# A GLA tile's output: turned by VectorE and stored by four transfers in place of TensorE, and the first out products in blocks of three

## The chip, the core and the metric

The kernel runs on one core of a Trainium2 chip. A core has five engines that run their own instruction queues beside each other: TensorE (PE in the profile, with its weight loads as PEld), VectorE (DVE), ScalarE (ACT), GpSimd (POOL) and SyncE (SP), which here issues nearly all DMA transfers. The metric is the device time of one execution in microseconds; a kernel's time is the median of its runs.

## The reference

One layer of a hybrid decoder, for a prompt of 2048 positions and 8 x 8 sampled positions, in float32. What bears on the change:

```
h    = RMSNorm(x);  proj = h @ w_in          # split into attention and GLA columns
attn = sliding-window attention with sinks    # 512 columns
# gated linear attention (GLA): 4 heads, dk 64, dv 128, log decays log_a per position and key
o    = causal GLA output, S = state carried from position to position
o    = rms_norm(o, g_gla) * silu(gr)          # per head of 128 columns
mix  = concat([attn, o]) @ w_out              # 1024 x 1024
x    = x + rms_norm(mix, g_mix_post)
x    = x + rms_norm((relu(RMSNorm(x) @ w_up))^2 @ w_down, g_ffn_post)
```

## The kernel before

The prompt is cut into tiles of 128 positions, 0 to 15; tile 16 (`NB`) holds the 64 sampled positions. Every float32 product is made of three products of float32r parts (high x high, high x low, low x high), so an operand is split before it is used: ACT copies the high part, DVE subtracts it for the low part.

The stages follow each other on TensorE: attention tiles (to about 310 us), GLA tiles (to about 670), output projection of the remaining tiles (to about 830), then the two MLP halves. The change is in the GLA stage and at its border to the output projection.

**A GLA tile.** `gla(i, gp, og)` is a generator. It computes decays with ACT and DVE (`level_sums`), weights keys and queries by them (`weighted_keys`, `weighted_queries`), has PE multiply them level by level into `gl` and `gh`, has DVE place those into a matrix AH under masks (`put_level`), copies that into AT, and has PE form the output from AT and the values and from the old state S (`o<-gp,AT`, `o<-S,qd`, and the same into the bank `ds`). The keys weighted to the tile's end (`kdT`) are turned by DVE in blocks of 32 x 32 and by way of memory: `keys_turn` transposes the blocks into `blocks`, stores four parts to `kd_d` and loads `kd` back. The next tile's queries and keys are turned in the same manner (`turn`).

**What runs between.** Each `yield n, free` of `gla` lets PE run n matmuls out of a long generator `fill`: the input projections of later tiles (`gproj`, by `products`), and at its end the first products of the output projection (`out`). The list `G_FILL` says how many stand at each place. `te`, `ac`, `dv` and `sq` wrap an engine so that its instructions stay in the order in which the program issues them; `sq` is SP's queue.

**The tile's output.** `finish_out(i, ...)` runs inside the next tile, `gla(i + 1)`, which steps it by `next(og)` and empties it by `deque(og, 0)`: squares on ACT, the inverse root on POOL, four DVE instructions into `og` (positions x columns). The output projection needs columns on partitions, so `og` is transposed: four PE transposes into a PSUM bank of kind "e" (`ogT`), an ACT copy to `mo`, one store to `mix_d[i][:, 4:8]`. The bank of kind "e" is also the one that the next tile's `o` takes. Tiles 15 and 16 do it in a branch of their own.

**The border to the output projection.** `products` ends with tile 15's projection, chunk by chunk. When a chunk of w_in has been used for the last time, its place takes parts of w_out: `load_wo` issues the loads of `wo` for columns 0 to 511, and after the last chunk `load_wo_half` those for columns 512 to 1023, two gains and `mt_raw`, the mix tile of tile 1. The parts of w_out were split and stored to `wo_d` in earlier tiles, one of eight per tile (`split_wo`, instructions `wop<-wor`). Mix tiles 0 and 4 (`B_ORDER[:2]`) are placed at the first chunk, and `split_mix(..., True)` puts their high parts into the list `highs` and their low parts, in halves, into `lows`; `gla` takes from these lists at fixed places with `take`. Then `out_projecting` for the two tiles runs in turns of two products:

```python
order[: 3 * KT] = [
    (0, k, u) for s in range(KT + 4) for k, u in ((s, 0), (s, 1), (s - 4, 2)) if 0 <= k < KT
]
```

so the products that need the low part of a mix tile (u = 2) come four k behind the others. The other mix tiles are loaded by `load_mix` and split by one ACT and one DVE instruction.

Of the kernel before, what the change touches and what calls it, by code (L numbers as in the profile page):

```python
# [12 lines left out]
F32 = mybir.dt.float32  # L13
F32R = mybir.dt.float32r
U8 = mybir.dt.uint8
AF = mybir.ActivationFunctionType
ALU = mybir.AluOpType
# [4 lines left out]
P = 128  # L22
D = 1024
KT = D // P
T = 2048
NB = T // P
# [54 lines left out]
B_ORDER = (*(j + b for j in range(4) for b in (0, 4)), NB, *(j + b for j in range(4) for b in (8, 12)))  # L81
# [47 lines left out]
def f32(ap):  # L129
    return ap.bitcast(F32)  # L130
# [23 lines left out]
def hybrid_step_kernel(ctx: ExitStack, tc: tile.TileContext, I, O):  # L154
# [10 lines left out]
    def rows(i):  # L165
        return min(P, NTOK - i * P)
# [7 lines left out]
    te, ac, dv, sq = (InOrder(tc, engine) for engine in (nc.tensor, nc.scalar, nc.vector, nc.sync))  # L174
# [17 lines left out]
    mix_d = [dpool.tile([P, KT, rows(i)], F32, name=f"mix_d{i}") for i in range(NTILE)]  # L192
# [36 lines left out]
    def split_copy(hi, lo, src, vector=nc.vector):  # L229

        nc.scalar.activation(hi, src, AF.Copy)
        return vector.tensor_tensor(lo, src, f32(hi), op=ALU.subtract)  # L232
# [52 lines left out]
    sp = open_pool("a_s")  # L285
# [583 lines left out]
    early, late = (deque((c, k) for c in cs for k in range(KT)) for cs in (G_EARLY, G_LATE))  # L869
# [21 lines left out]
    for i in range(NB):  # L891
# [21 lines left out]
        if i >= NB - 2:  # L913
            t = i - NB + 2
# [121 lines left out]
    sp = open_pool("g_s")  # L1036

    def places(name, shape, n=1, kind=F32):
        return cycle([sp.tile(shape, kind, name=f"{name}{u}") for u in range(n)])
# [3 lines left out]
    AT = sp.tile([P, 4, P], F32, name="AT")  # L1043
    AH = sp.tile([P, 4, HD], F32, name="AH")
    kds = places("kd", [P, 256], 2)
    ogs, mos = places("og", [P, 4, P]), places("mo", [P, 4, P])
    XK = sp.tile([P, NL, 2, P], F32, name="XK")
    XQ = sp.tile([P, NL, 2, 2, P // 2], F32, name="XQ")
    sgs = places("sg", [P, 512])
# [116 lines left out]
    def weighted_keys(xk, dec, kt, l, b, vector):  # L1166

        if l:
            vector.tensor_tensor(pairs(xk[:, l], b, 0), pairs(dec[:, l], b, 0), pairs(kt, b, 0), op=ALU.mult)
# [51 lines left out]
    def put_diagonal(i, at, gp, n, vector=dv):  # L1221
# [7 lines left out]
        shape = [n, 4, HD]  # L1229
        vector.copy_predicated(at, dmsk[:n].unsqueeze(1).to_broadcast(shape), dg[:n].unsqueeze(2).to_broadcast(shape))  # L1230

    def finish_out(i, og_src, sg, n, kind):

        ssq = sp.tile([P, 4], F32, tag="ossq", name=f"ossq_{i}", bufs=2)
        junk = sp.tile([P, P], mybir.dt.bfloat16, tag="ojunk", name=f"ojunk_{i}", bufs=1)
        scalar, vector = (ac, dv) if i < NB else (nc.scalar, nc.vector)
        for h in range(4):
            scalar.activation(junk[:n], og_src(h), AF.Square, accum_out=ssq[:n, h : h + 1])
            if i < NB - 1 and h in (0, 1, 3):
                yield  # L1240
        rs = sp.tile([P, 4], F32, tag="ors", name=f"ors_{i}", bufs=2)
        rsqrt_mean(sp, rs[:n], ssq[:n], n, P, 4, vector)
        if i < NB - 1:
            yield
        if i == NB:
            yield 44, True
            yield 44, True
        og = next(ogs) if i < NB else gp_s[:, :512].rearrange("p (h d) -> p h d", h=4)
        for h in range(4):
            with tc.issue_after(put[0].ins) if i == NB else nullcontext():  # L1250
                vector.scalar_tensor_tensor(
                    og[:n, h, :], og_src(h), rs[:n, h : h + 1], sg[:n, h * P : (h + 1) * P],
                    op0=ALU.mult, op1=ALU.mult,
                )
        for _ in range(S_WAIT[0] if i == NB else 1):
            yield 34, True
        pt = bank([P, 4, P], kind, f"ogT_{i}")
        for h in range(4):
            te.transpose(pt[:, h, :n], og[:n, h, :], ident[:n, :n])
        if i == NB - 1:  # L1260
            hi, lo = late_mix
            dv.tensor_copy(hi, pt)
            dv.tensor_tensor(lo, pt, f32(hi), op=ALU.subtract)
        elif i < NB - 1:
            mo = next(mos)
            ac.activation(mo, pt, AF.Copy)
            sq.dma_start(mix_d[i][:, 4:8, :], mo)
        else:
            nc.scalar.activation(gp_s[:, :256].rearrange("p (h t) -> p h t", h=4), pt[:, :, :n], AF.Copy)
            sq.dma_start(mix_d[i][:, 4:8, :], gp_s[:, :256].rearrange("p (h t) -> p h t", h=4))  # L1270
# [15 lines left out]
    def gla(i, gp, og=iter(())):  # L1286
# [20 lines left out]
        for l, b in enumerate(LEVELS[3:6], 3):  # L1307
            level_sums(before, after, dec, l, b)
            next(diagonal, None)
            take(lows, l % 2)  # L1310
            if l > 3:
                next(og, None)
            yield next(fills), False
        for l in (1, 2, 3):
            weighted_keys(XK, dec, kt, l, LEVELS[l], dv)
        ac.activation(edge, before[:, :, HD - 1 :: HD], AF.Copy, scale=1.0 / 16)
        whole(kdT, after, 0)
        dv.tensor_tensor(kdT, kdT, kt, op=ALU.mult)
        take(lows, 1)
        take(x_loads)  # L1320
        if i < NB - 1:
            keys_turn(i, kdT, kd)
# [8 lines left out]
        for l in (0, 1):  # L1331
            weighted_queries(XQ, dec, qz, l, LEVELS[l], dv)
        next(og, None)
        take(lows)
        yield next(fills), False
        level_sums(before, after, dec, NL - 1, LEVELS[-1])
        whole(dec[:, NL], before, 1)
# [28 lines left out]
        take(put_off)  # L1366
        yield next(fills), False
        deque(og, 0)
        yield next(fills), True
        yield next(fills), True  # L1370
        low = bank([P, 4, 4, P // 4], "c", f"gl_{i}")
# [38 lines left out]
        for g in range(2):  # L1410
            dv.scalar_tensor_tensor(
                Sn[:, g], So[:, g], dec[:, NL, g, P - 1 : P], ds[:, g], op0=ALU.mult, op1=ALU.add
            )
        yield next(fills), True
        for h in range(4):
            te.matmul(
# [99 lines left out]

    def split_mix(i, m, ks, raw, apart=False):
        n = rows(i)
        if apart:
            hi, lo = m[:, 1], m[:, 2]  # L1520
            highs.append(lambda: ac.activation(hi, raw, AF.Copy))
            for k in range(0, KT, 4):
                kk = slice(k, k + 4)
                lows.insert(
                    len(lows) if k else len(lows) // 2,
                    lambda kk=kk: dv.tensor_tensor(lo[:, kk], raw[:, kk], f32(hi[:, kk]), op=ALU.subtract),
                )
            return [[m[:, u, k, :n] for k in range(ks)] for u in (1, 2)]
        if i == NB:
            split_copy(m[:, 1, :, :NS], m[:, 1, :, NS:], raw[:, :, :NS])  # L1530
            return m[:, 1], None
        split_copy(m[:, 1, :ks, :n], m[:, 2, :ks, :n], raw[:, :ks, :n])
        parts = [[m[:, u, k, :n] for k in range(ks)] for u in (1, 2)]
        if i == NB - 1:
            for t, late in zip(parts, late_mix):
                t.extend(late[:, h, :] for h in range(4))
        return parts

    def load_mix(i):
        return split_mix(*place_mix(i))  # L1540

    def out_projecting(te, i, banks):

        mh, ml = mixes.pop(i, None) or load_mix(i)
        n, ends = 2 if i == NB else 3, range(2)
        order = [(c, k, u) for c in ends for k in range(KT) for u in range(n)]
        if i in B_ORDER[:2]:
            order[: 3 * KT] = [  # L1550
                (0, k, u) for s in range(KT + 4) for k, u in ((s, 0), (s, 1), (s - 4, 2)) if 0 <= k < KT
            ]
        elif i == B_ORDER[-1]:
            order = [(c, k, u) for k in range(KT) for c in ends for u in range(n)]
        for c, k, u in order:
            if k + u == 0:
                banks.append(bank([P, 512], "ab"[B_ORDER.index(i) % 2], f"out_{i}_{c}"))
            if i == NB:
                x, w = mh[:, k], wo[k][u]
            else:  # L1560
                x, w = (mh, mh, ml)[u][k], wo[k][u % 2]
            te.matmul(  # L1562
                banks[c], x, w[:, c * 512 : (c + 1) * 512], start=k + u == 0, stop=k == KT - 1 and u == n - 1,
            )
            yield
# [48 lines left out]
    def products():  # L1614

        xT = {G_NEXT[0]: first_xT}
        for i, after in zip(G_NEXT, (*G_NEXT[1:], None)):
# [6 lines left out]
            for c, ks in zip(G_ORDER, WO_PARTS):  # L1624
# [5 lines left out]
                if after is None:  # L1630
# [3 lines left out]
                    if c == G_ORDER[3]:  # L1634
# [3 lines left out]
                        raw = ss.tile([P, KT, P], F32, tag="part1", name="mt_raw", bufs=2)  # L1638
                        i = B_ORDER[2]
                        sq.dma_start(raw, mix_d[i])  # L1640
        early.extend((i, []) for i in B_ORDER[:2])
        first, second = (out_projecting(te, *e) for e in early)
        for _ in range(3 * KT // 2):
            yield from islice(first, 2)
            yield from islice(second, 2)
        yield from first
        m = gw[G_ORDER[0]][0].tile([P, 3, KT, P], F32R, tag=f"w{G_ORDER[0]}0", name=f"mt_{i}")
        mixes[i] = split_mix(i, m, KT, raw)
        i = B_ORDER[0]
# [30 lines left out]
    wo, pre, ogs_of, mixes, late_mix, g_mix, put, placing, x1_first = {}, {}, {}, {}, [], [], [], [], []  # L1680
    wo_parts = iter(())
    first_xT = load_T(G_NEXT[0], x_place(G_NEXT[0]), sq)
    early, x_loads, put_off, highs, lows, out_stage = [], [], [], [], [], []

    def take(waiting, n=None):
        for _ in range(len(waiting) if n is None else min(n, len(waiting))):
            waiting.pop(0)()
# [62 lines left out]
    sp = R["s"]  # L1750
# [139 lines left out]
    for n, i in enumerate(B_ORDER[2:]):  # L1890
# [3 lines left out]
        if n == 0:  # L1894
            first_rows = residual(*early.pop(0))
            next(first_rows)
            second = residual(*early.pop(0))
# [702 lines left out]
```

## Time and profile before

| | |
|---|---|
| runs | 2145.64, 2146.97, 2151.58 us (median 2146.97) |
| profiled execution | 2144.46 us, span of its records 2142.7 us |
| granted TensorE clock | 1.0 |
| PE busy | 2130.5 us, 99% of the span |
| DVE, ACT, POOL busy | 1522.4, 1217.3, 242.2 us |
| `ogT<-ident,og` on PE | 64 matmuls, 345.3 to 669.5 us |
| `mo<-ogT` on ACT | 15 of 577 ns (median) |
| `mix_d<-mo` on SP, in the GLA stage | 15 issues, 354.3 to 658.8 us |

Lines of a timeline have the start in us, the length in us, the engine, the source line, the operation, what it writes and reads by the program's names, the shapes and the number of instructions merged; in brackets stands the time that the engine sat idle before it and who released it. Line 143 is the wrapper through which all ordered instructions go. On SP a row is the issue of a transfer, not the transfer. In a table of windows each engine's busy time and its number of instructions follow the stretch.

### The profile page before, as it was taken

What the parts mean: (1) busy time and instruction counts of PE and PEld (TensorE: products, weight loads), DVE (VectorE), ACT (ScalarE), POOL (GpSimd) and SP (SyncE); (2) the same over time, 40 slices, a digit from 0 to 9 for tenths busy, and PEclk for the clock granted to TensorE, in tenths of its full rate; (3) what the DMA queues carried; (4) which work ended last, traced back from release to release, by engine and by line L of the source; (5) the groups of instructions that cost most, each with busy time, mean ns of one, the idle gap of its engine ahead of it and who ended that gap; (6) DMA issues with size and microseconds to landing.
All of it is one profiled execution on the core that took longest, in us unless ns stands there. A gap on an engine that the chain in (4) does not pass through costs nothing.

```text
span 2142.7 us, 34628 instructions
## 1 busy us (share of the span) xinstructions
PE 2130.5 (99%) x11888; PEld 1844.3 (86%) x11888; DVE 1522.4 (71%) x3167; ACT 1217.3 (57%) x2690; POOL 242.2 (11%) x407
## 2 busy tenths in 40 slices
PE   9999999999999999999999999999999999999998
PEld 9999999999997888888888888888888888888887
DVE  7998878777776666888887555558766666555576
ACT  7998867566764444655554554445454445544454
POOL 4676511111111100000000000000000000000000
PEclk9999999999999999999999999999999999999999
DMA  7444333545668568677786877668544443766685
GB/s 243 157 146 144 105 101 92 130 116 161 184 189 293 189 210 260 230 256 275 265 273 217 270 236 225 208 197 280 180 159 161 153 161 130 254 204 195 191 274 178
DMA packets 303133, 422.79 MB, mean 197 GB/s; under 512 B 79516, under 2 KB 204940, under 8 KB 298844
## 3 DMA queue, kind: packets, MB, share of 16 engines
q1 hardware_dynamic: 302796, 420.30, 60.5%
q8 instruction: 94, 1.54, 0.3%
q14 instruction: 83, 0.68, 0.1%
q10 hardware_dynamic: 160, 0.27, 0.0%
HBM read 271.39 MB, written 149.62 MB: 196 GB/s over the span
## 4 chain that ended last, share of the span: by engine, by line
PE 88%; DVE 5%; ACT 3%; DMA 2%; issue 1%; POOL 0%; SPq 0%; DVEq 0%; ACTq 0%; POOLq 0%
PE dn L143 28%; PE uc L143 8%; PE uX L143 8%; PE gproj L143 8%; PE out L1562 7%; PE proj L143 6%; PE ue L143 4%; PE ud L143 4%; PE ub L143 4%; PE dsam L143 1%; PE sam L143 1%; PE sc L143 1%; PE pT L143 1%; PE av L143 1%; PE out L143 1%
## 5 line engine op out<-in xcount | busy, mean ns | idle before, releaser
L143 PE MATMUL dn<-o0t,o1s 128*128 128x512 f32 x888 | 345.6, 389 | 0.0
L143 PE MATMUL dn<-o1t,o0s 128*128 128x512 f32 x888 | 345.5, 389 | 0.0
L143 PE MATMUL dn<-o0t,o0s 128*128 128x512 f32 x888 | 345.3, 389 | 0.0
L2224 DVE TENSOR_TENSOR o1s<-rs,o0s 128x512 fp32r<-128x512 f32 x224 | 154.6, 691 | 226.4 <-ACT o0s L2223 224.0
L2223 ACT ACTIVATE o0s<-rs 128x512 fp32r<-128x512 f32 x224 | 141.2, 631 | 294.3 <-PE dn L143 257.4
L143 PE MATMUL gproj<-wg,gxh 128*128 128x384 f32 x1024 | 271.3, 341 | 0.0
L143 ACT ACTIVATE st<-st 128x512 f32<-128x512 f32 x224 | 141.0, 630 | 102.2 <-DVE st L143 97.4
L143 PEld LDWEIGHTS dn<-o0t,o0s 128*128 128x128 f32 x888 | 166.7, 188 | 36.1 <-ACT f L2341 0.4
L143 PEld LDWEIGHTS dn<-o1t,o0s 128*128 128x128 f32 x888 | 166.7, 188 | 35.3
L143 PEld LDWEIGHTS dn<-o0t,o1s 128*128 128x128 f32 x888 | 166.7, 188 | 34.8
L143 PE MATMUL uc<-H,s 128*128 128x512 f32 x768 | 186.5, 391 | 1.1 <-ACT st L143 1.1
L143 PE MATMUL gproj<-wg,gxl 128*128 128x384 f32 x576 | 187.0, 342 | 0.3 <-DVE gp_s L143 0.3
L143 PEld LDWEIGHTS gproj<-wg,gxh 128*128 128x128 f32 x1024 | 184.1, 188 | 2.5 <-issue 2.1
L143 PE MATMUL uX<-H,w 128*128 128x512 f32 x768 | 185.1, 390 | 0.0
L143 PEld LDWEIGHTS uc<-H,s 128*128 128x128 f32 x768 | 143.0, 188 | 31.6 <-ACT st L143 1.3
L143 PEld LDWEIGHTS uX<-H,w 128*128 128x128 f32 x768 | 144.0, 188 | 30.3
L1562 PE MATMUL out<-wo,mt 128*128 128x512 f32 x680 | 158.6, 392 | 0.0
L2224 DVE TENSOR_TENSOR o1t<-rt,o0t 128x512 fp32r<-128x512 f32 x222 | 152.0, 686 | 1.7 <-ACT o0t L2223 1.7
L1562 PEld LDWEIGHTS out<-wo,mt 128*128 128x128 f32 x680 | 126.4, 188 | 26.2 <-DVE mt L232 0.2
L221 POOL TENSOR_TENSOR frs<-rs_v,half 128x1 f32<-128x1 f32 (+1 forms) x13 | 12.4, 960 | 1197.9 <-DVE rs_v L219 1197.9
L2223 ACT ACTIVATE o0t<-rt 128x512 fp32r<-128x512 f32 x222 | 137.0, 618 | 5.4 <-DMA rt<-t_d 3.7
L143 DVE TENSOR_TENSOR st<-st 128x512 f32<-128x512 f32 x160 | 110.6, 691 | 30.8 <-ACT st L143 26.5
(450 smaller groups left out, 4271.1 us busy)
## 6 DMA issues: line engine op xcount, KB each, us to landing
s_d<-st SPq DMA_DIRECT2D x32, 1792.0 KB
rs<-s_d SPq DMA_DIRECT2D x224, 256.0 KB
raw<-in_w_up SPq DMA_DIRECT2D x64, 512.0 KB
rt<-t_d SPq DMA_DIRECT2D x128, 256.0 KB
rt<-in_w_down SPq DMA_DIRECT2D x96, 256.0 KB
t<-in_w_down SPq DMA_DIRECT2D x64, 256.0 KB
t_d<-t SPq DMA_DIRECT2D x32, 512.0 KB
h_d<-ht SPq DMA_DIRECT2D x8, 1280.0 KB
```

The lines of the kernel that those rows point to most:

```text
L143: ins = call(*a, **k)
L221: return nc.gpsimd.tensor_tensor(out, v[:n], e, op=ALU.pow)
L1562: te.matmul(banks[c], x, w[:, c * 512 : (c + 1) * 512], start=k + u == 0, stop=k == KT - 1 and u == n - 1,)
L2223: high = nc.scalar.activation(hi, raw, AF.Copy)
L2224: low = nc.vector.tensor_tensor(lo, raw, f32(hi), op=ALU.subtract)
```

## The change

Tiles 0 to 14 no longer use PE, ACT and a PSUM bank for the transpose. When `finish_out` has written `og`, it leaves `out_turn` in a list `turning`. `out_turn` transposes `og` on DVE in blocks of 32 x 32 into a single buffer `turned` and issues four stores, one for each 32 partitions. The list is taken in the next tile, ahead of kdT's product and of `keys_turn`; tile 15 takes it a second time, behind `deque(og, 0)`, so that tile 14 is turned within tile 15 too. What lies in `mix_d[i][:, 4:8]` is permuted by this, and `split_mix` undoes the permutation while it splits: every mix tile is now split in two halves of four k, the second by a rearranged order of reading and writing.

The special order of the first products is dropped, and the two first tiles run in turns of three products, so that a k's product with the low part directly follows its two others. For that `gla` takes two of `lows` at the end of a tile already; two later places are dropped. (`l % 2` and `l != 4` give the same for l = 3, 4, 5.)

```diff
-    ogs, mos = places("og", [P, 4, P]), places("mo", [P, 4, P])
+    ogs, turned = places("og", [P, 4, P]), sp.tile([P, 4 * P], F32, name="turned")
...
+    def out_turn(i, og):
+
+        dv.transpose(turned.rearrange("t (a h x) -> t h a x", a=4, h=4), og.rearrange("x h (a t) -> x h a t", a=4))
+        for c in range(4):
+            src = turned[c * 32 : c * 32 + 32].rearrange("t (a e) -> t a e", a=4)
+            sq.dma_start(mix_d[i][:, 4 + c, :].rearrange("(a t) e -> t a e", a=4), src)
+
     def finish_out(i, og_src, sg, n, kind):
...
+        if i < NB - 1:
+            turning.append(lambda: out_turn(i, og))
+            return
         for _ in range(S_WAIT[0] if i == NB else 1):
             yield 34, True
...
-        elif i < NB - 1:
-            mo = next(mos)
-            ac.activation(mo, pt, AF.Copy)
-            sq.dma_start(mix_d[i][:, 4:8, :], mo)
...
-            take(lows, l % 2)
+            take(lows, l != 4)
...
         for l in (1, 2, 3):
             weighted_keys(XK, dec, kt, l, LEVELS[l], dv)
+        take(turning)
         ac.activation(edge, before[:, :, HD - 1 :: HD], AF.Copy, scale=1.0 / 16)
         whole(kdT, after, 0)
         dv.tensor_tensor(kdT, kdT, kt, op=ALU.mult)
-        take(lows, 1)
...
-        take(lows)
         yield next(fills), False
...
         deque(og, 0)
+        if i == NB - 1:
+            take(turning)
         yield next(fills), True
...
+        take(lows, 2)
         yield next(fills), True
...
-        split_copy(m[:, 1, :ks, :n], m[:, 2, :ks, :n], raw[:, :ks, :n])
+        for k in range(0, ks, 4):
+            kk = slice(k, k + 4)
+            hi, lo, src = m[:, 1, kk], m[:, 2, kk], raw[:, kk]
+            if k:
+                hi, lo = (t.rearrange("p h (c x) -> p h c x", c=4) for t in (hi, lo))
+                src = src.rearrange("p c (h x) -> p h c x", h=4)
+            if apart:
+                highs.append(lambda hi=hi, src=src: ac.activation(hi, src, AF.Copy))
+                lows.insert(
+                    len(lows) if k else len(lows) // 2,
+                    lambda hi=hi, lo=lo, src=src: dv.tensor_tensor(lo, src, f32(hi), op=ALU.subtract),
+                )
+            else:
+                split_copy(hi, lo, src)
...
-        if i in B_ORDER[:2]:
-            order[: 3 * KT] = [
-                (0, k, u) for s in range(KT + 4) for k, u in ((s, 0), (s, 1), (s - 4, 2)) if 0 <= k < KT
-            ]
-        elif i == B_ORDER[-1]:
+        if i == B_ORDER[-1]:
...
-        for _ in range(3 * KT // 2):
-            yield from islice(first, 2)
-            yield from islice(second, 2)
+        for _ in range(KT):
+            yield from islice(first, 3)
+            yield from islice(second, 3)
```

More of the change, by code (lines that the diff above doesn't have):

```diff
@@ L1518, in split_mix @@
         n = rows(i)
[L1519 to L1528, printed above, removed]
         if i == NB:
@@ L1682, in hybrid_step_kernel @@
     first_xT = load_T(G_NEXT[0], x_place(G_NEXT[0]), sq)
-    early, x_loads, put_off, highs, lows, out_stage = [], [], [], [], [], []
+    early, x_loads, put_off, turning, highs, lows, out_stage = [], [], [], [], [], [], []
     def take(waiting, n=None):
```

## The prediction

> **What bounds the kernel now.** First the page's line of engine shares.
>
> ```profile
> PE 2130.5 (99%) x11888; PEld 1844.3 (86%) x11888; DVE 1522.4 (71%) x3167; ACT 1217.3 (57%) x2690; POOL 242.2 (11%) x407
> ```
>
> PE is full almost everywhere, so a PE instruction that disappears is worth its pitch, unless another engine sets the pace where it stood. The stage of the GLA tiles therefore has to be read by itself, by a table of windows: two middle tiles, the last tile with the first out products, and the output-projection stage behind it (us, then busy time of PE, PEld, DVE, ACT, POOL, then clock, DMA share, GB/s).
>
> ```profile
> 588.00:609.00 21.00, 20.84 (x185) 20.02 (x184) 16.53 (x50) 14.37 (x47) 2.60 (x3) 1.00 0.59 173
> 641.00:670.00 29.00, 28.11 (x193) 22.19 (x192) 18.62 (x55) 13.94 (x49) 4.30 (x4) 1.00 0.88 312
> 670.00:830.00 160.00, 160.00 (x759) 133.00 (x758) 102.48 (x155) 69.25 (x140) 17.04 (x29) 1.00 0.65 213
> ```
>
> A tile takes 21 us; PE has small holes in the later ones. Behind 670 PE has none, and DVE and ACT are loose there. The clock is full throughout.
>
> **The TensorE transposes.** PE's timeline around one group of four, in a tile of the second half:
>
> ```profile
> 608.07 0.34 PE L143 MATMUL gproj<-wg,gxl 128*128 128x384 f32 x1
> 608.24 0.60 PE L143 MATMUL ogT<-ident,og 128*128 128x128 f32 x4
> 608.60 0.60 PE L143 MATMUL gproj<-wg,gxh 128*128 128x384 f32 x2
> 609.04 0.34 PE L143 MATMUL gproj<-wg,gxl 128*128 128x384 f32 x1
> 609.21 0.51 PE L143 MATMUL gproj<-wg,gxh 128*128 128x384 f32 x2
> 609.56 0.33 PE L143 MATMUL gproj<-wg,gxl 128*128 128x384 f32 x1
> ```
>
> Three projection products take 609.56-609.04 = 0.52 us; with the group among them the same three take 609.04-608.07 = 0.97. So a group costs 0.45 us of PE, not the 0.60 of its row, and fifteen cost 6.8 us. That is the most the removal can give by itself.
>
> Can PE use it? Matmuls that end a tile read AT, which DVE and ACT make. ACT's last write of AT, PE's first use of it, ACT's waits for PE, and two of DVE's rows:
>
> ```profile
> 468.63 0.41 ACT L143 ACTIVATE AT<-AH 64x256 f32<-64x256 f32 x1
> 471.01 0.38 PE L143 MATMUL o<-gp,AT 128*128 128x128 f32 x2
> 516.28 0.58 ACT L143 ACTIVATE gp<-gproj,rstd_all 128x384 f32<-128x384 f32 x1 [0.75 <-PE gproj L143]
> 605.28 1.28 DVE L143 SCALAR_TENSOR_TENSOR wop<-wor,ggla,wop 128x1024 fp32r<-128x1024 f32 x1 [1.67 <-ACT wop L143]
> 611.20 0.71 DVE L143 STREAM_TRANSPOSE blocks<-gp 128x512 f32<-128x512 f32 x1
> 614.43 0.32 PE L143 MATMUL o<-S,qd 64*64 64x128 f32 x1 [0.24 <-ACT mo L143]
> 618.08 0.41 ACT L143 ACTIVATE AT<-AH 64x256 f32<-64x256 f32 x1
> 618.66 0.38 PE L143 MATMUL o<-gp,AT 128*128 128x128 f32 x2
> ```
>
> In tile 6 AT is ready at 469.04 and used at 471.01: 1.97 us of slack. In tile 13 it is ready at 618.49 and used at 618.66: 0.17. From tile 7 on each tile also splits a part of w_out (wop), and the loop of DVE and ACT has become the pace; the last wait of ACT for PE in it is at 516.28, in tile 9, and PE already waits 0.24 for mo's copy in tile 13. So PE's gain is passed on to DVE and ACT only up to 516: groups of seven tiles (1 to 7; I leave tile 0's out, as the least certain), 7 x 0.45 = 3.2 us. The six groups of tiles 8 to 13 (2.7 us) and the waits for mo turn into a wait for AT. Ends for the gain up to tile 13: 0 and 6.8 plus a microsecond of those waits; I take 3.2.
>
> **What replaces them.** Each of 15 tiles gets a DVE transpose of 128x512: 0.71 us by the row at 611.20, of the same form. It is queued ahead of kdT's product, and a few rows behind it DVE sits 1.67 us waiting for ACT's part of wop (605.28), which hangs on nothing that DVE does in between. That covers it: nothing. Without that cover it is 0.71 a tile (rival D). ACT loses the mo copy, which delays only PE's o<-S; that wait goes, and the wait for AT comes later instead. SP issues four stores a tile in place of one, a step earlier in the next tile, ahead of the four kd stores:
>
> ```profile
> 624.42 1.74 SPq L143 DMA_DIRECT2D kd_d<-blocks  x4
> 625.73 1.61 DMA kd_d<-blocks
> 627.48 0.93 SPq L143 DMA_DIRECT2D kd<-kd_d  x2
> 634.82 0.61 PE L143 MATMUL ds<-gp,kd 128*64 128x128 f32 x8
> ```
>
> Four issues take 1.74 us; 0.87 of it runs beside kdT's product and transpose, so kd comes about 0.9 later. It is loaded by 628.41 plus some 1.6 and used at 634.82, so some 4 us are spare: nothing.
>
> In the output stage twelve mix tiles are split by two instructions of 128x512 each on ACT and DVE, half of them in a permuted order, instead of one of 128x1024. It lies behind PE's 160 of 160 busy us, with 57 us of DVE free: nothing. Uncovered, twice 0.68 (DVE's 128x512 at 653.71, below) against 1.28 (its 128x1024 at 605.28) would be 0.08 each, 1 us in all (an estimate).
>
> **The first out products.** PE, then SP's queue, where w_out's parts (wo) come in, then sizes from the list of DMA issues:
>
> ```profile
> 640.84 3.01 PE L143 MATMUL out<-wo,mt 128*128 128x512 f32 x12
> 644.42 0.50 PE L143 MATMUL out<-wo,mt 128*128 128x512 f32 x1 [0.57 <-DMA wo<-wo_d]
> 645.09 1.19 PE L143 MATMUL out<-wo,mt 128*128 128x512 f32 x4 [0.17 <-DMA wo<-wo_d]
> 646.43 4.87 PE L143 MATMUL out<-wo,mt 128*128 128x512 f32 x20 [0.15 <-DMA wo<-wo_d]
> 658.85 3.70 PE L143 MATMUL out<-wo,mt 128*128 128x512 f32 x15
> 662.38 0.38 PE L143 MATMUL o<-gp,AT 128*128 128x128 f32 x2
> 635.09 0.32 SPq L143 DMA_DIRECT2D mix_d<-mo  x1
> 636.54 19.93 SPq L143 DMA_DIRECT2D wo<-wo_d  x26
> ...
> 658.83 0.32 SPq L143 DMA_DIRECT2D mix_d<-mo  x1
> ```
>
> ```profile
> wo<-wo_d SPq DMA_DIRECT2D x32, 256.0 KB
> x_first<-in_x_prompt SPq DMA_DIRECT2D x1, 512.0 KB
> out_gla_prompt<-S SPq DMA_DIRECT2D x4, 32.0 KB
> ```
>
> A product takes (662.38-658.85)/15 = 0.235, at most. From 640.84 to 646.43 seventeen take 5.59 where 3.9 would do: 1.7 us of waiting for wo. In blocks of three a k lasts six products (1.4 us) instead of four; a part of 256 KB comes every 0.67 us (the waits for one k's two parts end at 644.42 and 645.09), 1.3 a k: the waits go. But the second halves of wo arrive at the same 1.3 a k and are then used at three products a k (0.7 us), so PE, earlier, meets them: of the 1.7 I give back 1.0 (ends 0 and 1.7). The vector's differences moved to the end of tile 14 fall where DVE idles for the queries' transposes; nothing. So without a new wait PE comes to tile 15's AT earlier by 3.2, by 0.45 (tile 13's group), by 0.45 (tile 14's) and by 0.7: 4.8 us, at 657.6.
>
> **The wait that is added.** There is one buffer `turned`. Tile 14 is turned within tile 15, half a tile behind tile 13, so DVE has to wait until tile 13's four stores have read it. Those are queued on SP behind everything that the end of the projections issues: the 26 wo loads, the gains and mt_raw. In the trace of before mo of tile 14 stood at that very place, at 658.83. Queued behind the waiting DVE are tile 15's masks, AT, and behind AT PE itself. DVE and ACT there, and the DMA's drain:
>
> ```profile
> 653.71 0.68 DVE L143 SCALAR_TENSOR_TENSOR sg<-gp,sg 128x512 f32<-128x512 f32 x1
> 657.24 1.58 DVE L143 COPY_PREDICATED AH<-c,gl 128x128 f32<-128x128 uint8 x4 [2.85 <-PE gl L143]
> 660.11 0.41 ACT L143 ACTIVATE AT<-AH 64x256 f32<-64x256 f32 x1
> 665.00:666.00 1.00, 1.00 (x6) 0.82 (x5) 0.34 (x2) 1.00 (x3) 0.55 (x1) 1.00 0.76 256
> 666.00:667.00 1.00, 1.00 (x6) 0.83 (x5) 1.00 (x3) 0.23 (x1) 0.36 (x1) 1.00 0.16 42
> ```
>
> DVE is ready to turn tile 14 at 654.4. The masks to AT's last write take 660.52-657.24 = 3.28. The DMA engines are busy until about 665.9; behind tile 14's store x_first and gla_prompt's rows were issued, 640 KB, two and a half parts of 0.67 us, so that store's data were through at about 664.2, and 0.5 more for its completion (my choice between 0 and 1.61) gives 664.7. In the new kernel everything there moves: -3.2 (the loop), +0.9 (the four stores ahead of kd delay the loads that follow), -0.7 (tile 13's 256 KB no longer ahead of the train): -3.0. So tile 13's stores are done at 661.7, tile 14 is turned at 662.4, AT is written at 665.7. PE has waited since 657.6, 8.1 us, and goes on 3.3 us later than before's 662.38. Nothing behind it has slack to return: 670 to 830 is PE alone.
>
> Bounds: without the queue of data (four issues to 660.6, 1.61 to land, less 3.0) AT is written at 663.2: +0.8. With the completion of 1.61 us and no shift of the train at all: 665.8+4.0-662.38 = +7.4. I take the value nearest the store that stood there.
>
> The rule that speaks to this stands in the Trainium skill, "DMA: Bandwidth & Descriptors", Anatomy of one DMA: a semaphore fires only once the last byte is confirmed landed, which makes most of some 2.0 us fixed per DMA. The 1.61 us of kd_d's stores are the nearest row and lie a little below it; with 2.0 in place of my 0.5 the sum would be +4.8.
>
> **The sum.** 2142.70 (span) + 1.76 (its run took 2144.46) + 3.3 = 2147.8. The runs' median, 2146.97, lies 2.5 above that execution, so on the median's scale 2150.3.
>
> **Rivals.**
> B: the loop of DVE and ACT is no pace at all and passes on all of PE's gain. For it: DVE is only 16.5 of 21 us busy. Against: AT's slack shrinks from 1.97 to 0.17 while no engine in the loop waits for PE. Then SP's train and tile 13's stores also move 3.8 more, and the end is at 3.3-3.8 = -0.5: 2146.5.
> C: the stores of tile 13 are through before DVE needs the buffer, or the wait is covered. For it: mo of tile 13 went at 635.09, ahead of the train. Against: the order of the code, which puts the new stores behind it. Then 4.8 are gained, 2142.2, and with B's gain about 8.6: 2138.4.
> D, the other side: the 0.71 us of DVE is not absorbed, since in tiles 7 to 14 DVE and ACT are the pace. Eight tiles give 5.7 on top of 3.3: +9.0, 2156.0. It decides from the point where DVE's wait for wop is below 0.71; the row shows 1.67.
> The Trainium skill's page "VectorE: DVE Perf Modes", The three transpose paths and the rules under it, sends a 128x128 transpose to TensorE where PSUM will do and says that VectorE turns blocks of 32x32 only; by it the change takes work from the wrong engine, which is D's result; the 1.67 us of waiting speak against it here.
>
> **How the numbers follow.** A (as summed) 0.55, B 0.12, C 0.17, D 0.16. A measurement of this kernel tells 0.3%, 6.4 us. C with the full gain and some unseen gain: faster 0.13. D and A's upper end: slower 0.22. Same 0.65. The likeliest alone spans 2147.8 to 2154.4; the range takes in C's smaller gain and D: 2141 to 2156.
>
> **What would show it.** Right: in tile 15 a DVE row turned<-og that waits some 10 us (651.2 to 661.7) for mix_d<-turned, PE's o<-AT waiting some 8 us behind it; o<-S waits for mo gone; a wait of PE for AT in tiles 10 to 13; DVE's wait for wop down to about 1.0. Wrong: tile 13's stores standing ahead of the wo loads in SP's queue; PE's tiles at 20.5 us up to the end (B); DVE's wop waits at zero (D).

## The result and the profile after

The changed kernel took 2153.53 us (median of 12 runs, 2151.96 to 2156.46) against 2146.57 us before (2144.74 to 2151.58): a ratio of 1.0032, 95% interval 1.0023 to 1.0041. It is 7.0 us slower, about the 0.3% that a measurement of this kernel can tell; 2150.3 was forecast. The profiled execution has a span of 2151.7 us.

The engine shares of the profile after show what was removed and that it did not pay:

```profile
PE 2129.1 (99%) x11828; PEld 1840.4 (86%) x11828; DVE 1530.6 (71%) x3195; ACT 1211.5 (56%) x2690; POOL 240.7 (11%) x407
```

Sixty matmuls are gone from PE, and DVE has 8 us more; ACT has as many instructions as before. PE is busy 1.4 us less, in a span that is 9.0 us longer.

**Where to measure.** All of the edit but the split by halves lies in the GLA stage and at its border, so a clock for that stretch alone is wanted: from PE's first product with AT in tile 1 to the first `out` product that the next stage issues. In PE's timeline before these are

```profile
356.00 0.49 PE L143 MATMUL o<-gp,AT 128*128 128x128 f32 x2
...
554.99 0.38 PE L143 MATMUL o<-gp,AT 128*128 128x128 f32 x2
...
639.60 0.38 PE L143 MATMUL o<-gp,AT 128*128 128x128 f32 x2
...
669.54 12.08 PE L1562 MATMUL out<-wo,mt 128*128 128x512 f32 x52
```

(tiles 1, 10 and 14; tile 15's row at 662.38 stands in the prediction), and after the change

```profile
357.52 0.49 PE L143 MATMUL o<-gp,AT 128*128 128x128 f32 x2 [0.41 <-DVE S L143]
...
553.32 0.49 PE L143 MATMUL o<-gp,AT 128*128 128x128 f32 x2 [0.16 <-ACT AT L143]
...
637.71 0.49 PE L143 MATMUL o<-gp,AT 128*128 128x128 f32 x2
...
656.64 3.01 PE L143 MATMUL out<-wo,mt 128*128 128x512 f32 x12
660.35 1.01 PE L143 MATMUL out<-wo,mt 128*128 128x512 f32 x3 [0.70 <-DMA wo<-wo_d]
668.81 0.79 PE L143 MATMUL o<-gp,AT 128*128 128x128 f32 x2 [7.44 <-DVE S L143]
...
670.53 7.23 PE L143 MATMUL out<-wo,mt 128*128 128x512 f32 x26
677.96 4.36 PE L1569 MATMUL out<-wo,mt 128*128 128x512 f32 x18
```

The stretch went from 669.54 - 356.00 = 313.54 us to 677.96 - 357.52 = 320.44: +6.9, which is the whole difference of the medians. (Tile 1 starts 1.5 later in this profile. That offset is no effect of the edit: among the runs below it lies between -0.9 and +3.7, and it was +2.0 in one whose program is the old one up to tile 7.) The rows split the 6.9: from tile 1 to 10 PE gains 3.2, from 10 to 14 only 0.2; in tile 15 it loses 8.3, and behind it 2.0 more. The output stage behind the border, with its split by halves, costs nothing here: to the first product of the MLP (`xnT`) it takes 160.80 us (677.96 to 838.76), before 160.81 (669.54 to 830.35).

**The wait.** The chain of waits of the profile after, around tile 15 (start us, us, what):

```profile
654.71 6.12 DMA wo<-wo_d
...
660.85 3.99 DMA mix_d<-turned
...
664.91 0.71 DVE turned L143
...
668.16 0.62 DVE S L143 x2
...
668.81 0.79 PE o L143 x2
```

It is the forecast wait: the loads of w_out, then tile 13's stores behind them, then the transpose of tile 14, the masks, AT, PE. DVE's and SP's timelines of the same place:

```profile
664.91 0.71 DVE L143 STREAM_TRANSPOSE turned<-og 128x512 f32<-128x512 f32 x1 [13.25 <-DMA mix_d<-turned]
...
634.92 20.79 SPq L143 DMA_DIRECT2D wo<-wo_d  x26
...
658.12 9.29 SPq L143 DMA_DIRECT2D mix_d<-turned  x8
```

**What the wait leaves behind.** PE's idle time is put down to S, the last of DVE's instructions; the chain shows that AT's place behind the transpose is the cause. Behind the wait PE is also slower: 26 `out` products took 7.23 us, 6.16 in the profile before, and the four pairs with AT 1.72 (668.81 to 670.53) where before they took 0.81 (662.38 to 663.19). The windows tell why; the third number from the right is the granted clock:

```profile
661.00:662.00 1.00, 0.37 (x2) 0.06 (x1) 0.00 (x0) 0.00 (x0) 0.00 (x0) 1.00 1.02 390
662.00:663.00 1.00, 0.00 (x0) 0.00 (x0) 0.00 (x0) 0.00 (x0) 0.00 (x0) 0.79 0.85 271
663.00:664.00 1.00, 0.00 (x0) 0.00 (x0) 0.00 (x0) 0.00 (x0) 0.00 (x0) 0.50 0.18 57
...
672.00:673.00 1.00, 1.00 (x4) 0.81 (x3) 0.17 (x1) 1.00 (x4) 0.38 (x1) 0.59 0.02 8
673.00:674.00 1.00, 1.00 (x6) 0.79 (x6) 0.33 (x2) 0.89 (x3) 0.63 (x1) 1.00 0.00 0
```

The 0.79 puts the fall to half at about 662.6, some 1.2 us after PE's last product (661.36); the 0.59 puts the return at about 672.8, 4.0 us after PE took up work. The Trainium skill, "TensorE: Matmul & The Clock Gate", Part 1, says that the clock is at half after at least one idle window of about 3.4 us and full after a busy one of that length, and that these windows run freely. The return agrees. The fall does not: in the 3.4 us that end at 662.6 PE still worked for some 1.5 (up to 659.65, and from 660.35 to 661.36), so no wholly idle window of that length lies ahead of it. What made it fall so early is not shown.

### The profile page after: what moved, and what is told of

Same layout as the page of the kernel before. It is cut to its first block, busy times and chain, and to the rows that moved or that the text cites. A ratio compares the mean times of both kernels' runs of the same rounds, so it can differ in the third digit from the quotient of the medians.

```text
span 2151.7 us, 34589 instructions
## 1 busy us (share of the span) xinstructions
PE 2129.1 (99%) x11828; PEld 1840.4 (86%) x11828; DVE 1530.6 (71%) x3195; ACT 1211.5 (56%) x2690; POOL 240.7 (11%) x407
## 3 DMA queue, kind: packets, MB, share of 16 engines
q8 instruction: 93, 1.52, 0.3%
## 4 chain that ended last, share of the span: by engine, by line
PE 83%; DVE 6%; DMA 4%; ACT 4%; issue 1%; SPq 0%; POOL 0%; DVEq 0%; ACTq 0%; POOLq 0%
PE dn L143 26%; PE uc L143 8%; PE uX L143 8%; PE out L1569 7%; PE proj L143 6%; PE gproj L143 6%; PE ue L143 4%; PE ud L143 4%; PE ub L143 4%; DMA wo<-wo_d 1%; PE sam L143 1%; PE sc L143 1%; PE dsam L143 1%; PE pT L143 1%; PE av L143 1%
```

## The experiments

The theory before them: (1) the single buffer makes a wait of 7 to 8 us in tile 15; (2) idleness of PE costs 2 us of half clock on top; (3) a loop of DVE and ACT paces the late tiles, so that the removed transposes give only 3 us; (4) the order in threes is worth under 1 us. Each run was timed beside the kernel before. Runs are set against each other by the stretch defined above.

| run | median us | ratio to before, 95% interval | stretch, us against before |
|---|---|---|---|
| changed kernel | 2153.53 | 1.0032 [1.0023, 1.0041] | +6.9 |
| other_buf | 2143.23 | 0.9982 [0.9974, 0.9991] | -3.0 |
| early13 | 2145.80 | 0.9992 [0.9983, 1.0000] | -0.5 |
| fill | 2157.58 | 1.0049 [1.0036, 1.0063] | +10.7 |
| fill32 | 2153.35 | 1.0029 [1.0018, 1.0040] | +5.0 |
| buf_pairs | 2145.01 | 0.9988 [0.9979, 0.9996] | -3.0 |
| threes | 2146.77 | 0.9994 [0.9985, 1.0004] | +0.1 |
| buf_double | 2144.43 | 0.9991 [0.9982, 0.9999] | -1.0 |
| buf_pool | 2147.05 | 1.0002 [0.9993, 1.0011] | +0.7 |
| buf_later | 2140.72 | 0.9971 [0.9960, 0.9981] | -6.0 |
| before_later | 2146.40 | 0.9997 [0.9988, 1.0005] | 0.0 |
| buf_later_dbl | 2145.09 | 0.9990 [0.9981, 0.9999] | -1.9 |

### The wait: another buffer (other_buf), or earlier stores (early13)

```diff
-        dv.transpose(turned.rearrange(...), og.rearrange(...))
+        place = blocks if i == NB - 2 else turned
+        dv.transpose(place.rearrange(...), og.rearrange(...))
...                                            # the stores read from place too
```

> Tile 14 is turned into the buffer of the queries' transposes (`blocks`, unused by then) instead of `turned`. Theory W (the loss is the wait of DVE for tile 13's stores): DVE no longer waits 13.2 us, PE no longer waits 7.4 us for AT in tile 15, and the clock, 0.50 for ten us after that wait, stays at 1.0, which is worth some 2 us more (26 out products took 7.23 us there and 6.16 before). So 2153.5 - 9.4 = 2144.1 us, 2 us under the kernel before. Rival L (the load of DVE's added transposes or the order of the first products costs the time): AT's wait is not what decides and the time stays above 2150 us.

The wait is gone from DVE's timeline. PE's rows in tile 15:

```profile
659.37 0.50 PE L143 MATMUL out<-wo,mt 128*128 128x512 f32 x1 [0.28 <-DMA wo<-wo_d]
659.70 0.38 PE L143 MATMUL o<-gp,AT 128*128 128x128 f32 x2
660.51 6.16 PE L143 MATMUL out<-wo,mt 128*128 128x512 f32 x26
```

AT is used at 659.70 without a wait, and the 26 products are back at 6.16. One more buffer for one tile is worth 9.9 us in the stretch (-3.0 against +6.9): 7.4 of stall, 2.0 of slow products, and 0.5 of the rest, of which 0.4 are shorter waits for wo. Point 1 is shown.

In early13 the wait is avoided by turning tile 13 in its own half of tile 14, with the one buffer:

```diff
-        if i == NB - 1:
+        if i >= NB - 2:
             take(turning)
```

> One buffer as in the changed kernel, but tile 13 is turned and stored within tile 14 already, where the old kernel stored it, ahead of the 26 loads of w_out's parts. Theory W: tile 14's transpose finds the buffer free, as with another buffer: 2144 to 2146 us; the 256 KB ahead of the loads cost at most 0.7 us. If the wait were not for the place of these stores in SP's queue but for one buffer as such (stores slow to land anywhere), DVE would still wait several us in tile 15 and the time would stay above 2148 us.

The stores now stand ahead of the 26 loads of w_out:

```profile
633.89 2.82 SPq L143 DMA_DIRECT2D mix_d<-turned  x4
637.11 19.86 SPq L143 DMA_DIRECT2D wo<-wo_d  x26
```

DVE no longer waits for the buffer, so the place of the stores in SP's queue, and not the single buffer as such, made the wait. But PE waits 1.8 us for wo (1.0 in other_buf), 0.96 at 648.39 the longest, and the stretch is 2.5 us longer than in other_buf, where at most 0.7 was expected for the 256 KB ahead of the loads. The time alone, 2145.80, lies in the expected range.

### The clock: dummy products in the wait (fill, fill32)

Products of the identity with itself, into a part of PSUM that nothing reads, ahead of tile 15's products with AT: 65 of them, then 32.

```diff
...                                         # oe_ is the whole bank that o_ is a part of
+        if i == NB - 1:
+            for _ in range(65):            # fill32: range(32)
+                te.matmul(oe_[:, 2], ident, ident, start=False, stop=True, skip_group_check=True)
```

> The changed kernel with 65 products of the identity with itself into an unused half of a PSUM bank, put in PE's queue ahead of tile 15's products with AT. They leave the result alone. At 0.11 us each they fill 7.2 of the 7.4 us that PE waits. Theory W with the clock: AT comes at the same time, but the clock stays at 1.0, so the products behind it take 6.2 instead of 7.2 us and those with AT 0.8 instead of 1.7: 2153.5 - 2.0 = 2151.5 us. Rival: the slower products are contention or a wait of their own and not the clock: 2153.5 us.

This run missed its size: each float32 product is recorded as two matmuls of 0.113 us, so the 65 took 14.7 us, and PE came to AT (675.38) 7.0 us after it was written (668.43). What it still shows is that the 26 `out` products behind them took 6.17. With 32:

> The changed kernel with 32 identity products of 128x128 ahead of tile 15's products with AT, into a part of the bank that nothing reads. The run with 65 showed that each is recorded as two matmuls of about 0.113 us, so 32 take about 7.2 us, just the wait for AT, and the granted clock stayed at 1.00 behind them. Theory (the wait costs 7.4 us and its idleness another 2 us of half clock): with the wait as long as before and the clock up, the AT products take 0.8 us and the 26 out products 6.2 instead of 7.2, so about 2 us less than the changed kernel, 2151.5. Rival (the slow products are not due to the idle engine, but to the operands or to the stores that run beside them): 2153.5 as the changed kernel, the 26 products at 7.2.

PE's rows:

```profile
660.36 7.30 PE L143 MATMUL o<-ident 128*128 128x128 f32 x64
667.98 0.49 PE L143 MATMUL o<-gp,AT 128*128 128x128 f32 x2 [0.32 <-ACT AT L143]
668.90 6.18 PE L143 MATMUL out<-wo,mt 128*128 128x512 f32 x26
```

From AT's first use to the end of the 26 products pass 7.10 us (667.98 to 675.08); before the change it was 6.97 (662.38 to 669.35), after it 8.95 (668.81 to 677.76). So in the profile point 2 is shown: the half clock cost 2.0 us, and work in the gap takes nearly all of it away. The times do not settle it: the medians of the two kernels differ by 0.2 us, and the intervals take in both 0 and 2 us.

### The order in threes (threes, buf_pairs)

threes is the kernel before with the changed order and the moved lows alone; its mix tiles are split as before. buf_pairs is other_buf with the old order of pairs. Of threes:

```diff
...                                             # the special order is dropped, lows are moved
-        for _ in range(3 * KT // 2):            # buf_pairs goes back to these three lines
-            yield from islice(first, 2)         # and to the special order
-            yield from islice(second, 2)
+        for _ in range(KT):
+            yield from islice(first, 3)
+            yield from islice(second, 3)
```

> The kernel before with only the other parts of the change: the first out products by blocks of three, the low parts at other places, the split of the output stage by halves as before; outputs turned by TensorE as before. Theory (1.7 us of waits for wo go, 1.0 comes back at the second half of the columns): 0.7 us less than before, 2146.3, within the bound of what can be told. Rival (the order is the source of the gain that the changed kernel shows with another buffer, 3 to 4 us): 2143 to 2144. Second rival (nothing comes back): 1.7 us less, 2145.3.

> The kernel with another buffer for tile 14, but the two first out tiles run in the old order (turns of two, the low part four k later). Theory: PE reaches tile 15's AT when the last parts of w_out that it needs have come, in either order (the changed kernel waits for them at 660.35 in the second column half), so the order is worth within 0.7 us of the other-buffer kernel, 2144 to 2145.5. Rival: the blocks of three save the 1.7 us of waits of the old order in full: 2145.8 or more.

Neither pair differs: +0.1 us in the stretch of threes, the same -3.0 in buf_pairs as in other_buf. (The median of buf_pairs is 1.8 us above that of other_buf, with overlapping intervals; in the profiles the two differ behind the border, where the output stage takes 162.46 us against 161.42.) PE's rows of threes show how the gain is undone within a tile:

```profile
642.07 4.75 PE L143 MATMUL out<-wo,mt 128*128 128x512 f32 x19
646.99 4.44 PE L143 MATMUL out<-wo,mt 128*128 128x512 f32 x18 [0.17 <-DMA wo<-wo_d]
...
656.21 0.45 PE L143 MATMUL gl<-XQ,qkT 128*64 128x64 f32 x8
...
659.01 3.58 PE L143 MATMUL out<-wo,mt 128*128 128x512 f32 x12
662.77 1.10 PE L143 MATMUL out<-wo,mt 128*128 128x512 f32 x3 [0.18 <-DMA wo<-wo_d]
```

Tile 15 began 1.22 us later than in the profile before; at 656.21 PE is only 0.17 behind it (there gl stood at 656.04), so 1.05 were gained at the first column half. Then the last 15 products ahead of AT take 4.71 us (659.01 to 663.72) where they took 3.53 (658.85 to 662.38): 1.18 given back at the second half, where the order uses up w_out faster than it comes; PE waits for wo there.

### The pace of the late tiles (buf_double, buf_pool, buf_later, before_later, buf_later_dbl)

Why does the gain stop at tile 10? All of these runs but before_later are other_buf with one or two more edits. In buf_double each transpose of `og` on DVE is done twice.

> The changed kernel with tile 14 turned into blocks, and each of VectorE's transposes of the 15 tiles done twice. Theory (the transpose lies in VectorE's waiting time: for ScalarE's half of w_out's split, or for TensorE): at most 1 us more than with blocks alone, 2143.2 to 2144.2. Rival D (VectorE's time is on the path that paces the tiles): 0.62 to 0.71 us for each of the tiles 6 to 14 at least, 5 to 8 us more, 2149 to 2151.

Two rows, DVE's waits from tile 1 to the border, in other_buf and then in buf_double (us in total, times, longest):

```profile
DVE wop L143 <- ACT wop L143: 10.8, 8, 1.5
```

```profile
DVE wop L143 <- ACT wop L143: 4.5, 8, 0.8
```

From tile 10 to 14 a tile takes 21.11 us with doubled transposes (552.88 to 637.31) and 21.13 without (552.18 to 636.71). The wait shrinks by 6.3 us and takes the second transposes in. The stretch is still 2.0 us longer, where at most 1 was expected: 0.75 from tile 2 to 3 (21.96 us against 21.21), where PE waits 0.81 for kd, and 1.4 in tile 15, where PE waits 2.2 for wo, 1.0 in other_buf. So in the late tiles the transpose isn't the pace, which does not yet say what is.

The first transpose went mostly into another wait. DVE's waits for ACT's part of kdT, whose product stands directly behind the transpose, from tile 1 to the border, before the change and then after it:

```profile
DVE kdT L143 <- ACT kdT L143: 6.0, 12, 1.1
```

```profile
DVE kdT L143 <- ACT kdT L143: 0.3, 1, 0.3
```

The wait for wop fell only from 11.6 us before to 10.8 after.

buf_pool takes the low part of w_out's split off DVE, in place of its two instructions there:

```diff
+            if k >= 4:
+                nc.gpsimd.tensor_tensor(raws[k], raws[k], ggla.to_broadcast([P, D]), op=ALU.mult)
+            ac.activation(parts[0], raws[k], AF.Copy)
+            nc.gpsimd.tensor_tensor(parts[1], raws[k], f32(parts[0]), op=ALU.subtract)
```

> The changed kernel with tile 14 turned into the buffer blocks, and with the low parts of w_out's split (wop, and from its fifth block on the product with the gain) on GpSimd instead of VectorE. Theory (from tile 10 on TensorE waits for AT, so the loop of VectorE and ScalarE sets the pace and the removed transposes give nothing more): VectorE loses 1.2 us of work and about 1.3 us of waiting for ScalarE's half per tile, so TensorE can go at its own pace to tile 14, 0.45 us per tile more: up to 3 us less than with blocks alone (2143.2), about 2140. Rival B (the loop is no pace, TensorE's own work is): 2143, no change. Second rival (GpSimd's work slows VectorE where both run): no gain or a loss, 2143 to 2148, with longer rows of VectorE beside GpSimd's.

The second rival won: the late tiles got longer, 22.25 us each from tile 9 to 13 (533.84 to 622.85) against 21.17 in other_buf (531.26 to 615.95). DVE's and POOL's timelines:

```profile
586.95 4.65 DVE L143 TENSOR_TENSOR XQ<-dec,qz 128x256 f32<-128x256 f32 x4
...
586.21 2.40 POOL L1601 TENSOR_TENSOR wop<-wor,wop 128x1024 fp32r<-128x1024 f32 x1 [0.33 <-POOL ors L221]
588.82 2.16 POOL L1599 TENSOR_TENSOR wor<-wor,ggla 128x1024 f32<-128x1024 f32 x1
```

Four DVE products that take 1.42 us in the other kernels take 4.65 while POOL runs beside them; they end 0.6 us behind POOL's second. The work left DVE's queue, but DVE stands still for it. (The Trainium skill, "SBUF — State Buffer", SBUF: two separate sides, describes this: a pair of ports that VectorE and GpSimd share, held for a whole instruction by the one that starts first, by VectorE when it reads two inputs from SBUF and GpSimd reads SBUF too. These rows agree.)

The chain of other_buf in a late tile is a closed loop of DVE and ACT without PE. Its part around w_out's split:

```profile
580.35 1.04 ACT wop L143
581.42 1.28 DVE wop L143
...
582.95 0.42 DVE XQ L143
583.37 1.04 DVE og L143 x4
```

DVE stands until ACT has written the high part, 581.42, then does the low part, and only then the XQ and og products, which need nothing of it. buf_later is other_buf with this order on DVE changed, and nothing else:

```diff
-        next(wo_parts, None)
         for l in (0, 1):
             weighted_queries(XQ, dec, qz, l, LEVELS[l], dv)
         next(og, None)
+        next(wo_parts, None)
```

> The changed kernel with tile 14 turned into blocks, and VectorE's low half of w_out's split (wop) put after the next XQ products and the og products instead of ahead of them; nothing else moves, the order on the other engines is the same. In the run with blocks alone the chain of waits of tiles 10 to 14 is a closed loop of VectorE and ScalarE of 21.25 us, in which VectorE stands 1.5 us for ScalarE's wop. Theory (that loop, through this wait, is why the transposes gain nothing from tile 10 on; the transposes themselves lie ahead of the wait): the wait goes, the loop falls below TensorE's own pace, and TensorE gains about 0.4 us in each of the tiles 10 to 14 too: 2 us less than with blocks alone (2143.2), 2141. Rival (the loop is paced elsewhere, or TensorE is): 2143, tiles of 21.2 us as before.

The chain in a late tile of buf_later (570 to 596 us), its shares by line:

```profile
by line: PE gproj L143 76.0%; PE gl L143 6.4%; PE o L143 5.9%; PE ds L143 5.5%; PE gh L143 5.3%; PE z L143 1.2%
```

Here it is PE from end to end, PE is busy for 82.0 of the 82.0 us from tile 10 to 14, and in PE's own timeline

```profile
359.69 0.49 PE L143 MATMUL o<-gp,AT 128*128 128x128 f32 x2 [0.38 <-DVE S L143]
...
555.38 0.38 PE L143 MATMUL o<-gp,AT 128*128 128x128 f32 x2
...
637.43 0.38 PE L143 MATMUL o<-gp,AT 128*128 128x128 f32 x2
...
667.25 12.06 PE L1570 MATMUL out<-wo,mt 128*128 128x512 f32 x52
```

tiles 10 to 14 take 20.51 us each. The stretch is 6.0 us shorter than before, near the 6.8 that the rows of the transposes promised. (Behind the border the output stage gives 1.0 back: 161.79 us against 160.81.) Theory 3 is shown from this side; the gain over other_buf is 3.0 in the stretch where 2 were expected. By the times alone the two intervals still overlap.

before_later is the control: the same move in the kernel before.

> The kernel before with only VectorE's wop put after the XQ and og products. Theory (in the kernel before TensorE's own work, transposes included, and the loop run at the same 21.2 us per tile, with 0.1 to 0.3 us of slack): no change, 2147 within 1 us. Rival (the wait for ScalarE's wop costs the kernel before too): 0.2 to 0.4 us in each of eight tiles, 2144 to 2145.

Nothing, 0.0 in the stretch. Tiles 10 to 14 do get a little shorter, 20.98 us each (557.03 to 640.93) against 21.15, and PE has no gap left in them: with its own transposes in, its work lies just below the loop. Tile 15 gives it back, 23.43 us against 22.78, with 1.4 us of waits for wo in place of 0.9. Neither edit alone reaches what both give.

buf_later_dbl doubles the transposes once more, now without the wait that hid them.

> The changed kernel with tile 14 turned into blocks, wop put later, and each of VectorE's transposes of the 15 tiles done twice. With the wait for ScalarE gone, VectorE's 0.62 us more lie on its own chain. Theory: the loop is back near TensorE's pace, so 0 to 0.3 us per tile in tiles 10 to 14: 0 to 1.5 us more than with wop put later alone, 2141 to 2143. Rival (the transpose is hidden wherever it stands, since other waits take it up): as wop put later alone, AT no later against TensorE than there.

The chain is again DVE and ACT, and the transposes are on it:

```profile
579.87 0.63 DVE turned L143
580.53 0.71 DVE turned L143
```

Tiles 10 to 14 take 20.98 us (554.24 to 638.17), 0.47 more than in buf_later, and the stretch is 4.1 us longer. The theory's size was too small (0 to 0.3 a tile, 1.5 in all), the rival wrong: with the cover gone, about two thirds of the added 0.7 us are paid for in each late tile.

## Why the prediction came out as it did

- **The gain.** 0.45 us for a group, handed on up to about tile 9 and then lost to the loop: 3.2 forecast, 3.2 measured between tiles 1 and 10. The pace was rightly named; buf_later shows it by taking it away. Rival B (no pace) falls. The further 1.6 that were summed up to tile 15's AT (two groups and the order) did not come: without the wait the stretch is 3.0 shorter (other_buf), not 4.8.
- **The transposes on DVE.** Absorbed in the late tiles, as forecast, but the step that names the cover was mostly wrong: not the wait for wop (11.6 us before, 10.8 after, still 1.5 in a late tile where 1.0 was forecast) but the nearer wait for kdT took them in, 6.0 us before and 0.3 after. The wop wait was the reserve: buf_double shows it holding a second transpose in the late tiles, buf_later_dbl shows the price without it. Rival D falls for this kernel. So does, as a guide here, the rule of the Trainium skill's page "VectorE: DVE Perf Modes", Rules for kernel authors, to turn 128x128 on TensorE where PSUM will do as the place of the result: TensorE is full, and 0.71 us on an engine that waits are cheaper than 0.45 on the one that doesn't. The term for kd, put at nothing from tile 14's 4 us to spare, was not nothing everywhere: in tile 3 PE waits 0.41 for it after the change, and before it did not wait.
- **The first out products.** 1.7 forecast, 1.0 given back; threes shows 1.05 and 1.18, so the net is nothing, not 0.7. The 1.7 took all of the row lengths above 0.235 a product for waiting; the waits in their brackets add up to 0.9. And a part of w_out was counted at 0.67 us from one gap, where the 26 issues took 19.93, 0.77 each.
- **The wait.** Place and cause as forecast. AT came 4.9 us later than before, counted from tile 1 (6.43 less the 1.52 of the start), where 3.3 was summed. The mis-sized term is the release of the buffer: tile 13's stores were done at 664.84, or 663.3 by the count from tile 1, and not at 661.7; from there to PE's start it took 4.0, as summed. The loads of w_out began 3.1 earlier by the same count (634.92 against 636.54, and the 1.52), as forecast, but their 26 issues took 20.79 us instead of 19.93, and the bulk of the data ended some 0.3 later than summed. The larger part, 1.3, is what follows: the DMA's share falls to 0.18 in the window from 663, so some 1.8 us lie between the bulk's end and the release, not 0.5. A trickle of data still runs in them (72, 43 and 18 GB/s in the half microseconds from 663.0), so how much of the 1.8 is completion stays open. The prediction's other sum, with the 2.0 us that the Trainium skill's "DMA: Bandwidth & Descriptors", Anatomy of one DMA, gives (for transfers that GpSimd issues; here it was SP), came to +4.8.
- **The step that was missing.** No term stood for the clock. After its stop of 7.4 us PE came back at a granted clock of 0.50, and that cost another 2.0 us. With it 4.9 + 2.0 make the measured 6.9.
- **The forecast itself.** Right in sign and mechanism, 3.2 us low: 1.6 from the release and 2.0 from the clock, less 0.4 because the median before is 2146.57 here and was 2146.97 there. The likeliest case's own range (2147.8 to 2154.4) still held it by the room given to the completion, which happened to be enough for the missing term too; so far it was luck.

## What to carry to other kernels

An instruction that waited for a store to leave its buffer waited here for the 26 loads that were queued ahead of that store; a second buffer for the one late tile was worth 9.9 us. Price such a wait on TensorE with its aftermath: the 7.4 us here brought 2.0 at half clock behind them. And when removed work stops paying, follow the chain of waits around one tile: here DVE and ACT set nearly the same pace as PE, and the second half of the gain lay in moving one DVE instruction behind others that did not need it.

buf_later, with tile 14 in another buffer and wop put later, is the best of these kernels: 2140.72 us, 0.9971 of the time before.

## What was not expected of the hardware

- A wait of 7.4 us on TensorE brought the granted clock to 0.50, and it was full again 4.0 us after work resumed; with products of 0.113 us in the gap it stayed at 1.00 (26 products took 6.18 us instead of 7.23).
- A float32 identity product of 128x128 is two matmul records, 0.23 us in all.
- Elementwise work of POOL beside DVE products of two inputs stretches these from 1.42 to 4.65 us.
- The last of four stores of 64 KB, behind a full queue, landed 3.99 us after its issue (660.85); the last of four stores of 32 KB within a tile (`kd_d<-blocks`) had taken 1.61.
